# In-projection of a streaming-encoder layer: p1 and p2 of four pairs ahead of the other operands, and the 1/rms spread between products

## The chip, the core and the metric

The kernel runs on one core of a Trainium2 chip. The metric is device time in microseconds (us) of one execution. The engines of the core run side by side, each with its own queue in a fixed order: TensorE (PE, matmul), VectorE (DVE), ScalarE (ACT), GpSimd (POOL) and SyncE (SP, which here only issues DMA transfers).

## The reference

One layer on x of 1024 frames by 1024 channels, all float32. The part that the change touches is the first: RMSNorm and the combined input projection.

```python
h    = rms_norm(x, norm_mix_pre)          # x / sqrt(mean(x^2) + eps) * gain
proj = h @ w_in                           # 1024 x 1024 times 1024 x 4096
q, k, v, u, gates = split(proj, [512, 1024, 1536, 2048], axis=-1)
y_a  = chunk_band_attention(q, k, v, rel_bias) @ w_attn_out
y_b  = multiscale_pool(u, w_pool_group, pool_scale) @ w_pool_out
g_a, g_b = split(sigmoid(gates + b_gate), 2, axis=-1)
x = x + rms_norm((g_a * y_a + g_b * y_b) @ w_o, norm_mix_post)
x = x + rms_norm(conv_gated_ffn(rms_norm(x, norm_ffn_pre), ...), norm_ffn_post)
```

## The kernel before

The 4096 output channels of the in-projection are 32 blocks of 128 (0 to 3 q, 4 to 7 k, 8 to 11 v, 12 to 15 u, 16 to 31 gates), taken two at a time as 16 pairs (`IN_PAIRS`). A matmul multiplies 128x128 of weights with 512 frames. Each float32 factor is split into a high and a low part (`split`, L77): ScalarE casts the high part (L78), VectorE subtracts it from the source for the low part (L79); the product then takes three matmuls (high·high, high·low, low·high), and with four slices of the inner dimension one product is 12 matmuls (`mm3`, L81).

Pairs 0 and 1 are computed plainly, from x that only carries the gain (tiles XR, products named i); their outputs are scaled by 1/rms when they are evicted (`evict_first`). For that ScalarE sums the squares of the rows (`squares`), small steps make 1/rms, and `spread` lays it out along the frames: a broadcast copy bc, four TensorE transposes into a PSUM bank (rps), a copy to the tile R0 or R1 (one for each half of the frames). Then `normalise` scales the four quadrants of x (q, in the trace xq) in place, four VectorE steps for a quadrant.

From pair 2 on, a pair is a 2x2 block product by a scheme with seven products instead of eight (`Pair`). They need these operands, each split into a high and a low tile of 128 x 2048 (`operand`, two steps of 128x1024 on ScalarE and two on VectorE): B11 for p1, B21 for p2, T1 for p5, T2 for p6, B22 for p3, T3 for p7, T4 for p4. T1 to T4 are made by `sub` from the quadrants, in place, in two VectorE steps each. On the weights' side, p5, p6, p3 and p7 use sums s1, s2, s4 and s3 of the raw blocks (`first`, `sums`, 128x512, on GpSimd); the weights of a product are split as well (wh, wl). p1 goes to the PSUM bank X, p6, p7 and p4 are added onto it there, and after p1, p6 and p7 something is read from it (copies c1, u2; evictions), so that the next product waits for that reading. p5 goes to bank Y, p3 is added onto it; p2 goes to Z. There are two banks of each name, and two named m.

Queues: code order, then a scheduler that sets the order on each engine once, by priority and its own estimates; in the trace every engine follows its queue. Raw weights (win) are loaded by SP into six buffers; pair 4's load takes the place of quadrant xq00, so it can be issued only when the last `sub`, which reads that quadrant, is done. After the in-projection come the pooled path, attention and the feed-forward block, which the change doesn't touch.

The printed lines below are those that the rows of the profile name. In the trace the buffer numbers are left out: X_i is bank X of any pair, wl_i any low weight, s_i any weight sum, i the plain products.

Of the kernel before, what the change touches and what calls it, by code (L numbers as in the profile page):

```python
# [17 lines left out]
P = 128  # L18
# [19 lines left out]
IN_PAIRS = (  # L38
    [(16 + m, 24 + m) for m in range(4)]
    + [(8, 9), (10, 11)]  # L40
    + [(12, 13), (14, 15)]
    + [(16 + m, 24 + m) for m in range(4, 8)]
# [5 lines left out]
def trunk(ctx, tc, xn, xt, w_in, cols, bias, w_ao, w_pg, w_po, w_o, gains, w_up, w_dn, out):  # L48
# [113 lines left out]
    class Pair:  # L162
# [3 lines left out]

        def __init__(self, raw, T, psp, tmp, name, evict, np_=6):
            w = raw.rearrange("p (f q k c) -> p f q k c", f=2, q=2, k=4)
            self.w11, self.w12, self.w21, self.w22 = w[:, 0, 0], w[:, 0, 1], w[:, 1, 0], w[:, 1, 1]
            self.T, self.psp, self.tmp, self.name, self.evict, self.np_ = T, psp, tmp, name, evict, np_  # L170

# [15 lines left out]
        def first(self):  # L187
            self.s1 = self.st("s1")
            G.tensor_tensor(self.s1, self.w21, self.w22, ALU.add)  # L189

        def sums(self):
            self.s2, self.s4, self.s3 = self.st("s2"), self.st("s4"), self.st("s3")
            G.tensor_tensor(self.s2, self.s1, self.w11, ALU.subtract)  # L193
            G.tensor_tensor(self.s4, self.w12, self.s2, ALU.subtract)
            G.tensor_tensor(self.s3, self.w11, self.w21, ALU.subtract)  # L195
# [12 lines left out]

        def p2(self):
# [4 lines left out]
        def p6(self):  # L214
            self.u2 = self.pt("u2")
            self.prod(self.X, self.s2, "T2", False, "6")
            A.copy(self.u2, self.X)

# [11 lines left out]
        def p4(self, last):  # L230
            X, c = (self.bank("Z"), self.c7) if last else (self.X, None)
            self.prod(X, self.w22, "T4", last, "4")
            self.evict(1, 0, X, c)
# [59 lines left out]
    with ExitStack() as ph:  # L293
# [73 lines left out]

        def half_in(pi, t, i, tag):


            for f in range(2):
                if i == 0:
# [10 lines left out]
        def squares(j):  # L383
            for t in range(4 * j, 4 * j + 4):
                A.activation(sq, xts[t], AF.Square, accum_out=ssq[:, t:t + 1])

        def spread(j):

            s = slice(4 * j, 4 * j + 4)
            rstd_of(rst[:, s], ssq[:, s], tmp, 4)  # L390
# [124 lines left out]

        def pair_in(n):
            return Pair(raws[n], T, psp, tmp, f"i{n}", evict_in(IN_PAIRS[n]))

        vds, pd = {}, None
        for pi, fb in enumerate(IN_PAIRS):  # L520
# [7 lines left out]
            if pi == 0:  # L528
# [24 lines left out]
                for j in range(2):  # L553
                    for i in range(2):
                        normalise(i, j)
                evict_first(0, 1)
            elif pi == 1:
                pair, nxt = pair_in(2), pair_in(3)
                operand("B11", q[0, 0])
                pair.p1()  # L560
                operand("B21", q[1, 0])
                pair.p2()
                evict_first(1, 1)
                pair.first()
                sub(q[0, 0], q[0, 1], q[0, 0])
                operand("T1", q[0, 0])
                nxt.p1()
                nxt.p2()
                pair.sums()
                pair.p5()  # L570
                sub(q[0, 0], q[1, 1], q[0, 0])
                operand("T2", q[0, 0])
                operand("B22", q[1, 1])
                sub(q[0, 1], q[1, 1], q[0, 1])
                operand("T3", q[0, 1])
                sub(q[1, 0], q[1, 0], q[0, 0])
                operand("T4", q[1, 0])
            else:
                after = nxt if pi == 2 else pair_in(pi + 1) if pi + 1 < len(IN_PAIRS) else None
                run_pair(pair, after, (), pi < 4)  # L580
                pair = after
            if 5 <= pi < 7:
                for b in IN_PAIRS[pi - 1]:
# [658 lines left out]
```

## Time and profile before

| | us |
|---|---|
| median of 3 runs (lowest, highest) | 1282.94 (1281.66, 1283.02) |
| the profiled execution | 1282.71 |
| its span, first to last instruction | 1280.9 |
| TensorE busy | 1245.8 |
| VectorE busy | 900.7 |
| ScalarE busy | 672.2 |
| GpSimd busy | 326.7 |

A matmul of 512 columns starts 0.227 us after the one before it when nothing is in its way, though its own record lasts 0.39 us, since matmuls overlap. A stretch in which TensorE is slow is therefore seen best by the number of matmuls in it: 90 in 20 us is full. The mean granted clock over the span is 0.994.

### The profile page before, as it was taken

Reading aid. Unit: us, or ns where it says so; the run is one execution under the profiler, and the core shown is the slowest. Engines: PE = TensorE matmul, PEld = TensorE weight load, DVE = VectorE, ACT = ScalarE, POOL = GpSimd, SP = SyncE. Lnnn points to the kernel's source line nnn. Section 1 sums busy time; section 2 is a strip of 40 time slices with the busy share of each in tenths; the row PEclk is TensorE's granted clock in tenths of the full one; section 3 lists DMA queues with packets and bytes.
Section 4 is the critical chain, followed back from the end, with each engine's and each line's share of the span. In section 5 each row is a group of like instructions: output and inputs, shape, how many; then the busy total and the mean of one; then the engine's idle time right before and its main releaser. Section 6 shows DMA issues by size and latency. Waiting matters only on the chain.

```text
span 1280.9 us, 16339 instructions
## 1 busy us (share of the span) xinstructions
PE 1245.8 (97%) x5780; PEld 1030.3 (80%) x5780; DVE 900.7 (70%) x1439; ACT 672.2 (52%) x1171; POOL 326.7 (26%) x278
## 2 busy tenths in 40 slices
PE   7969999999999999999999999999999999999997
PEld 6748888887788888888887888888888887888786
DVE  5883354685477777854789766766666666899958
ACT  7743344655377775433556455455555454445553
POOL 0132312323155656100033342343343310000000
PEclk9989999999999999999999999999999999999999
DMA  9252142234788964622233212222221249302003
GB/s 365 82 207 105 44 179 82 112 115 169 235 255 244 274 218 160 247 94 83 83 124 139 99 66 83 99 70 79 99 74 66 99 158 369 122 17 100 33 1 132
DMA packets 55569, 172.35 MB, mean 135 GB/s; under 512 B 5440, under 2 KB 6080, under 8 KB 50496
## 3 DMA queue, kind: packets, MB, share of 16 engines
q1 hardware_dynamic: 49136, 156.63, 35.4%
q10 hardware_dynamic: 4608, 8.39, 1.7%
q0 software_dynamic: 1744, 6.29, 1.3%
q8 instruction: 45, 0.74, 0.3%
q14 instruction: 36, 0.29, 0.1%
HBM read 124.11 MB, written 47.19 MB: 134 GB/s over the span
## 4 chain that ended last, share of the span: by engine, by line
PE 87%; DVE 7%; issue 3%; ACT 1%; DMA 1%; POOL 0%; DVEq 0%; SPq 0%; ACTq 0%; POOLq 0%
PE X_u L85 16%; PE X_i L85 10%; PE X L85 9%; PE Y_u L85 8%; PE wops L928 7%; PE Y L85 6%; PE Y_i L85 5%; PE Z_u L85 4%; PE y L85 4%; PE ybp L85 3%; PE u L85 3%; PE i L85 3%; PE f L742 2%; PE Z_i L85 2%; PE tp L717 2%
## 5 line engine op out<-in xcount | busy, mean ns | idle before, releaser
L1004 DVE SCALAR_TENSOR_TENSOR hc<-hu,cv,hc 128x1022 f32<-128x1022 f32 (+1 forms) x88 | 115.9, 1321 | 35.3 <-ACT hc L999 35.3
L78 ACT CAST wh_u<-s_u 128x512 fp32r<-128x512 f32 x80 | 49.5, 618 | 78.3 <-PE Y_u L85 38.1
L79 DVE TENSOR_TENSOR wl_u<-s_u,wh_u 128x512 fp32r<-128x512 f32 x80 | 57.1, 714 | 40.1 <-ACT wh_u L78 40.0
L189 POOL TENSOR_TENSOR s_u<-wup 128x512 f32<-128x512 f32 x20 | 36.5, 1824 | 172.8 <-DMA wup<-in_w_up 127.0
L79 DVE TENSOR_TENSOR wl_i<-s_i,wh_i 128x512 fp32r<-128x512 f32 x56 | 40.7, 729 | 55.6 <-ACT wh_i L78 55.6
L78 ACT CAST wh_u<-wup 128x512 fp32r<-128x512 f32 x72 | 44.6, 622 | 61.5 <-PE Y_u L85 28.9
L78 ACT CAST wh_i<-s_i 128x512 fp32r<-128x512 f32 x56 | 34.8, 621 | 61.5 <-PE X_i L85 27.1
L193 POOL TENSOR_TENSOR s_u<-s_u,wup 128x512 f32<-128x512 f32 x20 | 28.1, 1405 | 137.5 <-DVE wl_u L79 137.5
L999 ACT ACTIVATE hc<-hu,cv 128x1024 f32<-128x1024 f32 x44 | 54.6, 1244 | 10.6 <-DVE hu L989 8.1
L78 ACT CAST wh_i<-win 128x512 fp32r<-128x512 f32 x46 | 28.2, 622 | 48.7 <-PE X_i L85 32.7
L79 DVE TENSOR_TENSOR wl_u<-wup,wh_u 128x512 fp32r<-128x512 f32 x72 | 50.3, 700 | 4.8 <-PE tp L285 2.0
L195 POOL TENSOR_TENSOR s_u<-wup 128x512 f32<-128x512 f32 x20 | 45.4, 2272 | 30.6 <-DVE wl_u L79 30.6
L79 DVE TENSOR_TENSOR ptl<-tp,pth 128x512 fp32r<-128x512 f32 (+3 forms) x80 | 43.7, 555 | 13.6 <-ACT pth L78 12.2
L696 POOL TENSOR_SCALAR pe<-pe,st 128x640 f32<-128x640 f32 (+2 forms) x64 | 43.1, 676 | 33.1 <-DVE st L695 28.4
L693 ACT ACTIVATE pe<-sm,st 128x640 f32<-128x640 f32 (+2 forms) x64 | 44.6, 697 | 6.4 <-DVE st L691 5.5
L189 POOL TENSOR_TENSOR s_i<-win 128x512 f32<-128x512 f32 x14 | 19.7, 1406 | 104.7 <-DMA win<-in_w_in 58.3
L1009 ACT ACTIVATE hc<-hc 128x1024 f32<-128x1024 f32 x22 | 23.4, 1064 | 40.9 <-DVE hc L1004 40.9
L79 DVE TENSOR_TENSOR wl_i<-win,wh_i 128x512 fp32r<-128x512 f32 x46 | 32.6, 713 | 16.4 <-ACT wh_i L78 16.4
L691 DVE CUSTOM_DVE_ANT_0 sm<-pst,bt 128x640 f32<-128x640 f32 (+2 forms) x64 | 40.7, 651 | 4.0 <-PE pst L675 1.6
L85 PE MATMUL ybp<-mx,wh_yb 128*128 128x512 f32 x128 | 43.3, 418 | 0.0
L78 ACT CAST pth<-tp 128x512 fp32r<-128x512 f32 (+3 forms) x80 | 37.1, 472 | 9.1 <-PE tp L717 6.8
L193 POOL TENSOR_TENSOR s_i<-s_i,win 128x512 f32<-128x512 f32 x14 | 20.7, 1478 | 80.8 <-DVE wl_i L79 80.7
(498 smaller groups left out, 4219.0 us busy)
## 6 DMA issues: line engine op xcount, KB each, us to landing
wup<-in_w_up SPq DMA_DIRECT2D x22, 1024.0 KB, 5.1
win<-in_w_in SPq DMA_DIRECT2D x14, 1024.0 KB, 5.5
g_d<-hc SPq DMA_DIRECT2D x20, 512.0 KB, 2.6
sig_d<-d ACTq DMA_DIRECT2D x32, 256.0 KB, 2.0
a<-g_d SPq DMA_DIRECT2D x8, 1024.0 KB, 6.2
b<-in_w_dn SPq DMA_DIRECT2D x8, 1024.0 KB, 8.7
x<-in_xn SPq DMA_DIRECT2D x8, 512.0 KB, 12.7
v_d<-vt SPq DMA_DIRECT2D x8, 512.0 KB, 3.2
```

The source lines that it names most:

```text
L78: A.copy(hi, src)
L79: (eng or V).tensor_tensor(lo, src, hi.bitcast(F32), ALU.subtract)
L85: nc.tensor.matmul(ps, a[i], b[i], start=start and i == 0 and p == 0, stop=stop and i == n - 1 and p == 2, skip_group_check=True,)
L189: G.tensor_tensor(self.s1, self.w21, self.w22, ALU.add)
L193: G.tensor_tensor(self.s2, self.s1, self.w11, ALU.subtract)
L195: G.tensor_tensor(self.s3, self.w11, self.w21, ALU.subtract)
L691: V.tensor_tensor_reduce(so, sv, bv, -1.0, 3e38, ALU.add, ALU.min, st[:, 0:1])
L693: A.activation(pe[:, :n], sm[:, :n], AF.Exp, scale=-1.0, bias=st[:, 0:1], accum_out=st[:, 1:2])
L696: G.tensor_scalar(pe[:, :n], pe[:, :n], st[:, 2:3], 1.0, ALU.mult, ALU.mult)
L928: nc.tensor.matmul(ps[:, 512 * c:512 * c + 512], a[k // 4][:, k % 4, sl], wo[k][b][:, 512 * c:512 * c + 512], start=k == 0 and x == 0, sto ...
L999: A.activation(c, hu, AF.Identity, scale=cv[:, C_CW + 88 + b:C_CW + 89 + b], bias=cv[:, C_CB + b:C_CB + b + 1])
L1004: V.scalar_tensor_tensor(c[:, n:], hu[:, :S - n], cv[:, w:w + 1], c[:, n:], ALU.mult, ALU.add)
```

## The change

`IN_PAIRS` takes the u blocks as pairs 4 and 5 and the v blocks as pairs 6 and 7; before it was the other way round. For pairs 4 and 5 the first half of their weights (128x1024, what p1 and p2 need) is loaded a second time into tiles of its own (w12), and p1 and p2 of both are computed (`p12`) behind those of pairs 2 and 3, before p5 of pair 2. p1's result is kept in c1, a tile in SBUF; p6 of these pairs starts a new X bank, and VectorE adds c1 when p5, p6 and p4 are read. The whole weights of these pairs are loaded as before, and their other products run in their old place. The operands T1 to T4 and B22 are made between products. The weight sums of pairs 2 and 3 are made by VectorE, not GpSimd. All squares are summed before the first spread; the copy R of each spread is made by VectorE, not ScalarE; each spread stands behind one or two half products of pairs 0 and 1, and the quadrants of the first half of the frames are normalised between the two spreads. The transposes of the values (v) move with their pairs, from behind pairs 5 and 6 to behind pairs 7 and 8.

```diff
 IN_PAIRS = (
     [(16 + m, 24 + m) for m in range(4)]
+    + [(12, 13), (14, 15)]
     + [(8, 9), (10, 11)]
-    + [(12, 13), (14, 15)]
...
+        def p12(self, w, c1):
+            self.early, self.c1 = True, c1
+            w = w.rearrange("p (q k c) -> p q k c", q=2, k=4)
+            Z = self.bank("m")
+            self.prod(Z, w[:, 0], "B11", True, "1")
+            A.copy(c1, Z)
+            Z = self.bank("m")
+            self.prod(Z, w[:, 1], "B21", True, "2")
+            self.evict(0, 0, Z, c1)
...
             self.prod(self.Y, self.s1, "T1", True, "5")
-            A.copy(self.c5, self.Y)
+            if self.early:
+                V.tensor_tensor(self.c5, self.Y, self.c1, ALU.add)
+            else:
+                A.copy(self.c5, self.Y)
...
-            A.copy(Rb[j], ps)
+            V.tensor_copy(Rb[j], ps)
...
-                squares(0)
+                with tc.high_priority():
+                    for j in range(2):
+                        squares(j)
+                        scales(j)
+                half_in(0, 1, 0, "Z", (0,))
                 spread(0)
-                squares(1)
-                half_in(0, 1, 0, "Z")
-                spread(1)
                 for n in range(2):
                     evict_first(n, 0)
-                half_in(0, 1, 1, "Z")
+                half_in(0, 1, 0, "Z", (1,))
+                half_in(0, 1, 1, "Z", (0,))
+                for i in range(2):
+                    normalise(i, 0)
+                spread(1)
+                half_in(0, 1, 1, "Z", (1,))
...
-                pair, nxt = pair_in(2), pair_in(3)
+                pair, nxt = pair_in(2, V), pair_in(3, V)
+                wh = []
+                for n in (4, 5):
+                    w = tmp.tile([P, 1024], F32, tag="o", bufs=4, name=f"w12_{n}")
+                    nc.sync.dma_start(w, w_in[n][:, :1024])
+                    c = out_tile(f"c1_{n}")
+                    wh.append((w, c))
                 operand("B11", q[0, 0])
                 pair.p1()
                 operand("B21", q[1, 0])
                 pair.p2()
+                nxt.p1()
                 evict_first(1, 1)
-                pair.first()
                 sub(q[0, 0], q[0, 1], q[0, 0])
+                nxt.p2()
                 operand("T1", q[0, 0])
-                nxt.p1()
-                nxt.p2()
+                early = []
+                for n in range(2):
+                    p = pair_in(4 + n, None)
+                    p.p12(*wh[n])
+                    early.append(p)
+                    if n == 0:
+                        pair.first()
+                        sub(q[0, 0], q[1, 1], q[0, 0])
+                        operand("T2", q[0, 0])
                 pair.sums()
                 pair.p5()
-                sub(q[0, 0], q[1, 1], q[0, 0])
-                operand("T2", q[0, 0])
                 operand("B22", q[1, 1])
                 sub(q[0, 1], q[1, 1], q[0, 1])
+            elif pi == 2:
+                nxt.first()
+                pair.p6()
                 operand("T3", q[0, 1])
+                pair.p3()
                 sub(q[1, 0], q[1, 0], q[0, 0])
+                nxt.sums()
+                pair.p7(False)
                 operand("T4", q[1, 0])
+                nxt.p5()
+                pair.p4(False)
+                pair = nxt
```

How it moves the queues, at three places. The numbers in the names tell tiles apart; i2 to i5 are pairs 2 to 5, a leading digit is the product (wl_6_i2 is the low weight of p6 of pair 2).

VectorE, from the sixth operand on, before: T2, B22, T3 and T4 with the steps that make them, and in between the first low weight of p6 of pair 2.

```order
L79 TENSOR_TENSOR T2l_623<-xq00_103,T2h_622 128x1024 x2
L79 TENSOR_TENSOR B22l_629<-xq11_106,B22h_628 128x1024 x2
L424 TENSOR_TENSOR xq01_105<-xq11_106,xq01_105 128x1024 x2
L424 TENSOR_TENSOR xq10_104<-xq10_104,xq00_103 128x1024
L79 TENSOR_TENSOR T3l_637<-xq01_105,T3h_636 128x1024 x2
L424 TENSOR_TENSOR xq10_104<-xq10_104,xq00_103 128x1024
L79 TENSOR_TENSOR T4l_645<-xq10_104,T4h_644 128x1024
L79 TENSOR_TENSOR wl_6_i2_656<-s2_i2_595,wh_6_i2_655 128x512
L79 TENSOR_TENSOR T4l_645<-xq10_104,T4h_644 128x1024
L79 TENSOR_TENSOR wl_3_i2_673<-s4_i2_596,wh_3_i2_672 128x512
```

The same stretch of VectorE's queue now, from T2 on.

```order
L79 TENSOR_TENSOR T2l_642<-xq00_103,T2h_641 128x1024 x2
L476 TENSOR_TENSOR d12_0_634<-m_i4_617,c1_4_487 128x512
L79 TENSOR_TENSOR wl_2_i5_667<-w12_5_488,wh_2_i5_666 128x512
L201 TENSOR_TENSOR s3_i2_687<-win2_279 128x512
L79 TENSOR_TENSOR wl_5_i2_694<-s1_i2_637,wh_5_i2_693 128x512
L79 TENSOR_TENSOR B22l_711<-xq11_106,B22h_710 128x1024 x2
L476 TENSOR_TENSOR d14_0_682<-m_i5_665,c1_5_490 128x512
L453 TENSOR_TENSOR xq01_105<-xq11_106,xq01_105 128x1024 x2
L195 TENSOR_TENSOR s1_i3_720<-win3_281 128x512
L79 TENSOR_TENSOR wl_6_i2_724<-s2_i2_685,wh_6_i2_723 128x512
L79 TENSOR_TENSOR T3l_741<-xq01_105,T3h_740 128x1024 x2
L79 TENSOR_TENSOR wl_3_i2_747<-s4_i2_686,wh_3_i2_746 128x512
```

The low weights of p5, p6 and p3 of pair 2 now stand one after each operand; between them lie evictions of pairs 4 and 5 and weight sums that were GpSimd's.

TensorE, at the end of p2 of pair 3 (the bank Z_i3), before and, in the second block, now; m_i4 are the banks of p1 and p2 of pair 4.

```order
L85 MATMUL Z_i3_574<-B21l_511,wh_2_i3_575 128x512
L85 MATMUL Z_i3_574<-B21h_510,wl_2_i3_576 128x512
L85 MATMUL Y_i2_601<-T1h_549,wl_5_i2_604 128x512
L85 MATMUL Y_i2_601<-T1h_549,wh_5_i2_603 128x512
L85 MATMUL Y_i2_601<-T1l_550,wh_5_i2_603 128x512
```

```order
L85 MATMUL Z_i3_572<-B21l_517,wh_2_i3_573 128x512
L85 MATMUL Z_i3_572<-B21h_516,wl_2_i3_574 128x512
L85 MATMUL m_i4_599<-B11h_491,wh_1_i4_600 128x512
L85 MATMUL m_i4_599<-B11l_492,wh_1_i4_600 128x512
L85 MATMUL m_i4_617<-B21h_516,wh_2_i4_618 128x512
L85 MATMUL m_i4_617<-B21l_517,wh_2_i4_618 128x512
L85 MATMUL m_i4_599<-B11h_491,wl_1_i4_601 128x512
```

Where p5 of pair 2 came, p1 and p2 of pair 4 come, and behind them those of pair 5; 48 matmuls now stand ahead of p5 of pair 2.

SP, behind the loads of pairs 2 and 3, now; before, pair 4's load stood there first.

```order
L597 DMA w12_4_485<-in_w_in 128x1024
L597 DMA w12_5_488<-in_w_in 128x1024
L488 DMA u_d_69<-d12_0_634 128x512
L488 DMA u_d_69<-d14_0_682 128x512
L328 DMA win4_718<-in_w_in 128x2048
L328 DMA win5_838<-in_w_in 128x2048
```

Two half loads and two stores of u stand ahead of the load of pair 4.

## Rows read from the trace of the kernel before

**Rows 1.** The page: busy us, share of the span and instructions of each engine.

```profile
PE 1245.8 (97%) x5780; PEld 1030.3 (80%) x5780; DVE 900.7 (70%) x1439; ACT 672.2 (52%) x1171; POOL 326.7 (26%) x278
```

**Rows 2.** Windows: length, busy us (count) of PE, PEld, DVE, ACT, POOL; clock; DMA share, GB/s.

```profile
40.00:60.00 20.00, 19.77 (x89) 15.91 (x88) 18.36 (x30) 14.40 (x20) 1.29 (x1) 1.00 0.18 67
60.00:80.00 20.00, 12.37 (x48) 8.33 (x46) 20.00 (x21) 12.86 (x17) 2.16 (x1) 0.94 0.19 62
80.00:100.00 20.00, 15.75 (x62) 12.86 (x63) 13.55 (x16) 7.30 (x12) 12.21 (x8) 0.80 0.75 279
100.00:120.00 20.00, 20.00 (x90) 16.57 (x89) 6.64 (x10) 7.85 (x13) 5.93 (x5) 1.00 0.29 106
```

**Rows 3.** TensorE's waits, 0 to 340 us: total us, times, longest.

```profile
PE X_i L85 <- DVE wl_i L79: 9.4, 2, 9.2
...
PE Z_i L85 <- DVE wl_i L79: 1.2, 1, 1.2
```

**Rows 4.** Windows of 5 us; the clock is the third column from the end.

```profile
75.00:80.00 5.00, 0.07 (x1) 0.00 (x0) 5.00 (x5) 3.00 (x3) 0.00 (x0) 0.77 0.22 39
80.00:85.00 5.00, 0.75 (x2) 0.65 (x3) 5.00 (x6) 1.18 (x2) 0.63 (x1) 0.50 0.95 347
85.00:90.00 5.00, 5.00 (x18) 3.93 (x17) 3.16 (x5) 1.11 (x2) 4.92 (x3) 0.70 0.96 364
```

**Rows 5.** The chain that ended last, 0 to 130 us: start, us, what.

```profile
53.21 2.27 DVE B11l L79 x2
...
67.14 3.37 DVE xq L424 x2
...
83.59 0.61 DVE wl_i L79
...
101.25 2.72 PE Y_i L85 x12
```

**Rows 6.** TensorE in order of time: start, us, instruction, idle before and releaser.

```profile
33.22 0.60 PE L395 MATMUL rps<-ident,bc 128*128 128x128 f32 x4
...
44.85 0.60 PE L395 MATMUL rps<-ident,bc 128*128 128x128 f32 x4
...
84.25 0.79 PE L85 MATMUL X_i<-T2h,wl_i 128*128 128x512 f32 x1 [9.18 <-DVE wl_i L79]
...
88.36 0.40 PE L85 MATMUL Y_i<-B22h,wl_i 128*128 128x512 f32 x1
...
101.09 0.39 PE L85 MATMUL Y_i<-B22h,wh_i 128*128 128x512 f32 x1
```

**Rows 7.** VectorE, ScalarE and GpSimd in order of time, columns as above.

```profile
33.85 0.59 ACT L397 COPY R<-rps 128x512 f32<-128x512 f32 x1 [2.78 <-PE rps L395]
34.47 2.48 DVE L408 TENSOR_TENSOR d<-i,R 128x512 f32<-128x512 f32 x4 [4.15 <-ACT R L397]
36.87 3.17 DVE L402 SCALAR_TENSOR_TENSOR xq<-xq,cv,R 128x512 f32<-128x512 f32 x3
...
44.14 0.43 DVE L392 COPY bc<-rst 128x512 f32<-128x512 f32 x1
...
49.28 2.73 DVE L402 SCALAR_TENSOR_TENSOR xq<-xq,cv,R 128x512 f32<-128x512 f32 x4
...
67.27 2.16 POOL L189 TENSOR_TENSOR s_i<-win 128x512 f32<-128x512 f32 x1 [20.45 <-ACT wh_i L78]
...
75.57 3.48 DVE L424 TENSOR_TENSOR xq<-xq,xq 128x1024 f32<-128x1024 f32 x3
```

**Rows 8.** Loads and stores (us to landing); GpSimd's second sum (ns, min/median/max).

```profile
win<-in_w_in SPq DMA_DIRECT2D x5, 1024.0 KB, 5.3
...
x<-in_xn SPq DMA_DIRECT2D x8, 512.0 KB, 12.7
...
DMA to landing us min/median/max: 2.6/3.2/4.5
...
L193 POOL TENSOR_TENSOR s_i<-s_i,win x3: 1291/1298/3907, 35.5 to 93.3; 128x512 f32<-128x512 f32 x3
```

More of the change, by code (lines that the diff above doesn't have):

```diff
@@ L162, in trunk, with __init__, weights @@
     class Pair:
-        def __init__(self, raw, T, psp, tmp, name, evict, np_=6):
+        def __init__(self, raw, T, psp, tmp, name, evict, np_=6, eng=G):
+            self.early, self.eng = False, eng
+            self.weights(raw)
+            self.T, self.psp, self.tmp, self.name, self.evict, self.np_ = T, psp, tmp, name, evict, np_
+        def weights(self, raw):
+            if raw is None:
+                return
             w = raw.rearrange("p (f q k c) -> p f q k c", f=2, q=2, k=4)
             self.w11, self.w12, self.w21, self.w22 = w[:, 0, 0], w[:, 0, 1], w[:, 1, 0], w[:, 1, 1]
-            self.T, self.psp, self.tmp, self.name, self.evict, self.np_ = T, psp, tmp, name, evict, np_
         def st(self, n):
@@ L215, in p6 @@
             self.u2 = self.pt("u2")
-            self.prod(self.X, self.s2, "T2", False, "6")
-            A.copy(self.u2, self.X)
+            if self.early:
+                self.X = self.bank("X")
+            self.prod(self.X, self.s2, "T2", self.early, "6")
+            if self.early:
+                V.tensor_tensor(self.u2, self.X, self.c1, ALU.add)
+            else:
+                A.copy(self.u2, self.X)
         def p3(self):
@@ L230, in p4 @@
         def p4(self, last):
-            X, c = (self.bank("Z"), self.c7) if last else (self.X, None)
+            X, c = (self.bank("Z"), self.c7) if last else (self.X, self.c1 if self.early else None)
             self.prod(X, self.w22, "T4", last, "4")
@@ L366, in split_in, with half_in @@
                 ws[pi, f, i] = split_w(w[:, f, i], f"i{pi}_{i}{f}", None, place)
-        def half_in(pi, t, i, tag):
-            for f in range(2):
+        def half_in(pi, t, i, tag, fs=range(2)):
+            for f in fs:
                 if i == 0:
@@ L542, in trunk @@
                     split_raw(i, 1)
-                squares(0)
+                with tc.high_priority():
[3 more added lines that the diff above has]
+                half_in(0, 1, 0, "Z", (0,))
                 spread(0)
-                squares(1)
-                half_in(0, 1, 0, "Z")
-                spread(1)
                 for n in range(2):
                     evict_first(n, 0)
-                half_in(0, 1, 1, "Z")
+                half_in(0, 1, 0, "Z", (1,))
[4 more added lines that the diff above has]
+                half_in(0, 1, 1, "Z", (1,))
                 half_in(1, 1, 0, "Y")
                 half_in(1, 1, 1, "Y")
-                for j in range(2):
-                    for i in range(2):
-                        normalise(i, j)
+                for i in range(2):
+                    normalise(i, 1)
                 evict_first(0, 1)
             elif pi == 1:
-                pair, nxt = pair_in(2), pair_in(3)
+                pair, nxt = pair_in(2, V), pair_in(3, V)
[5 more added lines that the diff above has]
+                    wh.append((w, c))
                 operand("B11", q[0, 0])
@@ L562, in trunk @@
                 pair.p2()
+                nxt.p1()
                 evict_first(1, 1)
-                pair.first()
                 sub(q[0, 0], q[0, 1], q[0, 0])
+                nxt.p2()
                 operand("T1", q[0, 0])
-                nxt.p1()
-                nxt.p2()
+                early = []
[7 more added lines that the diff above has]
+                        operand("T2", q[0, 0])
                 pair.sums()
                 pair.p5()
-                sub(q[0, 0], q[1, 1], q[0, 0])
-                operand("T2", q[0, 0])
                 operand("B22", q[1, 1])
                 sub(q[0, 1], q[1, 1], q[0, 1])
+            elif pi == 2:
+                nxt.first()
+                pair.p6()
                 operand("T3", q[0, 1])
+                pair.p3()
                 sub(q[1, 0], q[1, 0], q[0, 0])
+                nxt.sums()
+                pair.p7(False)
                 operand("T4", q[1, 0])
-            else:
-                after = nxt if pi == 2 else pair_in(pi + 1) if pi + 1 < len(IN_PAIRS) else None
-                run_pair(pair, after, (), pi < 4)
+                nxt.p5()
+                pair.p4(False)
+                pair = nxt
+            else:
+                after = early[pi - 3] if 3 <= pi < 5 else pair_in(pi + 1) if pi + 1 < len(IN_PAIRS) else None
+                if after is not None and after.early:
+                    after.weights(raws[pi + 1])
+                run_pair(pair, after, (), pi < 6)
                 pair = after
-            if 5 <= pi < 7:
+            if 7 <= pi < 9:
                 for b in IN_PAIRS[pi - 1]:
```

17 lines of the change are left out of this document (10 added, 7 removed).

## The prediction

> **What bounds the kernel now.** I read the page's first two blocks first: TensorE is busy 97% of the span, so time can only come from the few places where it isn't [rows 1]. The table by 20 us shows the largest that the change touches: a full window of 20 us holds 90 matmuls, those from 60 and from 80 us hold 48 and 62, the second at a granted clock of 0.80 [rows 2]. The list of waits names VectorE as the releaser, above all one wait of 9.2 us for a weight's low part (wl) [rows 3]. The windows of 5 us show what that wait does beside it: granted clock 0.77, 0.50, 0.70 and then full again [rows 4]. The chain of waits says why: from 53 to 84 us the end is set almost only by VectorE, which makes operand after operand, two steps of 128x1024 at a time, and TensorE enters it for a few matmuls only; from 84.25 us on the chain is TensorE alone, 2.72 us for a product of 12 matmuls [rows 5]. So this block is VectorE's, and everything behind it TensorE's: what the block saves arrives at the end, as long as nothing later waits.
>
> How much is lost: from 55.07 us (first matmul of p1 of pair 2) to 101.09 us (first of p3 of pair 3) TensorE does 11 products, 132 matmuls. At 2.72/12 = 0.227 us each that is 29.9 us; it takes 46.0. **16.1 us are lost**, about 14.3 of them waiting and 1.8 at the half clock: the ten matmuls behind the long wait take 4.1 us (84.25 to 88.36) instead of 2.3 [rows 6].
>
> **The change part by part.** The order of TensorE's queue shows that p1 and p2 of pairs 4 and 5 now stand ahead of p5 of pair 2. They need only B11 and B21, so the same 11 products become 15 in the block, and four fewer have to run behind it. No matmul is added or removed. The comparison is thus: before, the same work ends at 101.09 + 4 x 2.72 = 111.97 us. Where does it end after?
>
> *Before the block.* The first spread's transposes (rps0) now stand behind 12 instead of 5 matmuls of the first half product, 7 x 0.23 = 1.6 us later: 33.2 + 1.6 + 0.6 = 35.4 us instead of 33.8 [rows 6]. The copy to R0 goes from ScalarE (0.59 us there) to VectorE. No row shows this copy on VectorE; the nearest are a broadcast copy of the same size (0.43) and an eviction from PSUM (0.62), I take 0.6 as it also reads PSUM [rows 7]. The Trainium skill, "VectorE: DVE Perf Modes", section "Why PSUM operands drop a tier", lets fp32 from PSUM run at one element a cycle, an estimate of 512 / 0.96 GHz = 0.53 us; by it the sum would be 0.1 us shorter, and no row here shows it. Behind R0 VectorE does four evictions (2.4), eight normalise steps (0.68 each beside no GpSimd work, 5.4; before, three of them took 3.17 us while GpSimd made a weight sum, which now is on VectorE), and some 1.1 of small steps up to bc1: 36.0 + 8.9 = 45.0 us. TensorE reaches rps1, now three matmuls later than before, at 44.85 + 0.7 = 45.5: no wait, with 0.5 us to spare. While it transposes, VectorE makes s1 and s2 of pair 2 (1.2), then copies R1 (0.6), makes s4 (0.6), eight normalise steps (5.4) and two evictions (1.2): **B11l begins at 54.0 us, where it began at 53.1** [rows 5, 7].
>
> *The block on VectorE.* From B11l to the low weight of p5 of pair 3 (wl_5_i3) its queue now holds 22 steps of 128x1024 (1.135 each, 25.0 us), 13 low weights, 8 evictions and 5 weight sums of 128x512 (26 x 0.61 = 15.8 us): 40.8 us. The sums on VectorE have no row either; a low weight is the same shape and also reads SBUF twice, so 0.61. Bounds: 0.57, half of a 128x1024 step, and 0.85, half of the slowest such step in the trace; eight sums, -0.3 to +2.0 us. They replace GpSimd's, and one GpSimd sum beside two operand steps took 2.16 us and held those up from 2.27 to 3.37 [rows 5, 7]: with GpSimd out of the block that delay goes too. So wl_5_i3 is ready at 54.0 + 40.8 = 94.8 us, if VectorE never waits.
>
> *Does VectorE wait?* Its steps that need TensorE or ScalarE, walked in the order of its queue: d18_0 (p2 of pair 2 ends at 62.2, VectorE is there at 62.6), d19_0 (66.7 and 67.3), d12_0 (73.1 and 74.3), d14_0 (78.5 and 79.0), d18_1 (88.1 and 88.9), d26_1 (93.1 and 93.6). It is there last each time, by 0.4 to 1.2 us. ScalarE is not bound: it has 0.95 us per 128x1024 cast against VectorE's 1.135, and loses to VectorE everywhere but at p5's copy, where p3 of pair 2 waits some 0.6 us for it.
>
> *TensorE through the block.* It waits for the first wl (57.0 instead of 56.1: 1.2 us in all, B11l's half included), 1.0 before p1 of pair 4, 0.6 and 0.4 at p3 and p6 of pair 2, 0.3, then 1.3 + 0.5 at p6 of pair 3 and p7 of pair 2, 1.2 at p4 of pair 2 behind d26_1; about 6 us in total, the longest piece 1.3. From wl_5_i3 on three stretches of ten matmuls are left up to p3 of pair 3 (5 of pair 3, 4 of pair 2, 6 of pair 3): 94.9 + 3 x 2.27 = **101.7 us against 111.97: 10.3 us gained.** Behind it VectorE has one low weight (0.6) for each 2.72 us of TensorE, plus an eviction.
>
> *Costed at nothing, and by what cover.* (a) The two half loads for pairs 4 and 5 are issued on SP when TensorE is done with the old tiles, at about 35 and 38 us, with the queues quiet by then (DMA share 0.18 from 40 us on) [rows 2]; they are needed at 67 us. (b) SP now has the u stores of d12_0 and d14_0 ahead of pair 4's load. That load waits for the last operand's subtraction anyway: issued at 88.3 instead of 78.0 us. With 5.3 us to land (the median of these five; 12.7 was the median of the eight x loads at the start), 1.3 for GpSimd's sum (up to 3.9), 0.6 and 0.7 for the split it is done at 96.2, at worst 106; p5 of pair 4 wants it at 101.7 + 5.4 = 107.1 [rows 7, 8]. Without this cover each us would count. (c) The added evictions (p5, p6, p4 of pairs 4 and 5 now add c1 on VectorE, six of 0.6 us) lie where VectorE is busy 7 of 20 us [rows 2]. (d) The values of pairs 6 and 7 now fall together with the pooled path's start, in pair 9: four splits, one low weight, two pooled steps of 1.2, an eviction, the next low weight, 7.3 us of VectorE, against five products (13.6 us) before p5 of pair 10 wants it.
>
> The profiled execution took 1282.71 us, span 1280.9; the median of the runs is 1282.94. 1282.9 - 10.3 = **1272.6 us**.
>
> **The rivals.** *Clock.* The block now has many short idles where it had one long one. The rows speak against a fall: from 56 to 75 us TensorE had waits up to 1.24 us and stayed at 1.00, and the level fell only in the wait of 9.2 us [rows 3, 4, 6]. The Trainium skill, "TensorE: Matmul & The Clock Gate", section "A second HAM failure mode: psum-queue depth-cycling", says that short and frequent idles between groups of matmuls can swing the clock between its two levels; the trace does not show that here. Where it happens, one fall costs 4.1 - 2.3 = 1.8 us as in the ten slow matmuls; one to two falls give 1274.4 to 1276.3.
>
> *Given back later.* If the cover of (b) or (d) fails: a store of values takes 3.2 us to land and frees a tile that the pooled path writes; one such wait inside pair 9, or a load that lands like those at the start, costs 1 to 4 us [rows 8]: 1273.6 to 1276.6.
>
> *VectorE is not faster without GpSimd.* If what slowed the two operand steps to 3.37 us and the three normalise steps to 3.17 was not GpSimd but the traffic around them, it can meet more steps in the fuller queue. If all were hit: 11 pairs of 128x1024 by 1.1, 16 normalise steps by 0.37, 21 sums and low weights by 0.3: 24 us, 1297 us. From 10.3 / 24 = 43% of them on nothing is gained, from 54% on the kernel is slower; a quarter of the way past that is some 1288. Against it: in the same trace three subtractions from 75.57 us take 3.48 (1.14 each) with ScalarE and DMA at work and GpSimd still [rows 7].
>
> *It doesn't do what it says.* The order of the queues excludes most of that; what could remain is that VectorE, not the products, sets the block, which is already the forecast.
>
> **How the numbers follow.** Forecast 0.68; clock 0.10; given back 0.08; VectorE slowed so that about nothing is left 0.08 (1280.5 to 1285.5); slowed further 0.06. A measurement of this kernel can tell about 0.2%, 2.6 us. Faster 0.68 + 0.10 + 0.08 = 0.86, same 0.08, slower 0.06. The forecast's own bounds are -0.3 to +2.0 for the sums, 0.4 for the copies, and about 1.5 either way for a walk in which waits of 0.4 us decide: 1270 to 1275.5. With the clock and the given-back cases the range is 1269.8 to 1277.8.
>
> **What would show it.** Right: no wait of TensorE over 2 us between 55 and 105 us, granted clock 1.00 in all windows from 60 to 100, VectorE without a gap from 54 to 94, wl_5_i3 near 95 us, p3 of pair 3 at 101 to 103 us after four more products; GpSimd idle until about 95; from 110 us on 90 matmuls in each 20 us. Wrong: VectorE idle in the block (a dependency that I walked wrongly), a window below clock 0.9, or operand steps above 1.2 us with GpSimd idle; behind the block, a wait at p5 of pair 4 or in pair 9.

## The result, and the profile after

The changed kernel takes **1274.75 us** (median of 4 runs, 1273.87 to 1275.48) against 1282.92 in the 4 runs of the kernel before beside it: ratio 0.9938, 95% interval 0.9921 to 0.9955. Five more runs of it, beside nine of before, gave 1274.74 us and 0.9937 (0.9925 to 0.9950). It is 8.2 us faster; 10.3 were forecast.

The profiled execution took 1275.48 us, span 1273.7. It is the longest of its four; the first profiled execution of the later set (a2 below) took 1273.87. Both are used, to tell what belongs to the program from what belongs to one execution.

The table by 20 us, columns as in [rows 2]:

```profile
40.00:60.00 20.00, 19.36 (x87) 15.54 (x86) 19.90 (x33) 12.62 (x17) 0.00 (x0) 1.00 0.25 90
60.00:80.00 20.00, 19.34 (x85) 15.69 (x85) 20.00 (x25) 12.99 (x20) 0.00 (x0) 1.00 0.17 66
80.00:100.00 20.00, 17.75 (x72) 12.69 (x72) 18.71 (x23) 9.86 (x15) 4.51 (x3) 1.00 0.75 265
100.00:120.00 20.00, 20.00 (x90) 16.58 (x89) 9.05 (x14) 8.03 (x13) 9.81 (x7) 1.00 0.46 166
200.00:220.00 20.00, 19.13 (x90) 15.40 (x89) 13.30 (x22) 10.25 (x18) 3.44 (x3) 1.00 0.61 227
220.00:240.00 20.00, 19.63 (x86) 15.85 (x85) 15.68 (x21) 11.68 (x20) 6.55 (x5) 1.00 0.36 136
```

The two windows that held 48 and 62 matmuls [rows 2] hold 85 and 72, the granted clock stays at 1.00, GpSimd (fifth pair of columns) is still up to 80 us, and VectorE is busy for 58.6 of the 60 us from 40 to 100. The last two rows are a place where TensorE is now busy 19.13 and 19.63 us of 20 (the 90 of the first take in transposes, which are shorter than a matmul of 512 columns). Before, nothing was lost there:

```profile
200.00:220.00 20.00, 20.00 (x90) 16.57 (x89) 6.82 (x11) 9.40 (x16) 4.24 (x4) 1.00 0.18 68
220.00:240.00 20.00, 20.00 (x90) 16.49 (x89) 12.74 (x18) 10.06 (x17) 6.51 (x4) 1.00 0.41 145
```

TensorE's waits from 0 to 340 us (total us, times, longest). The one of 9.2 us [rows 3] is gone. Apart from the wait for the first weights at the start of the program (7.5 us, 7.1 before), none is over 1 us:

```profile
PE X_i L85 <- DVE d L476: 1.8, 2, 0.9
PE X_i L85 <- ACT u_i L243: 0.9, 2, 0.6
PE X_i L85 <- ACT wh_i L78: 0.8, 1, 0.8
PE m_i L85 <- DVE wl_i L79: 0.7, 1, 0.7
PE X_i L85 <- DVE wl_i L79: 0.6, 1, 0.6
```

The chain of waits, 30 to 110 us (start, us, what). It answers [rows 5]:

```profile
54.46 2.27 DVE B11l L79 x2
...
69.04 6.29 PE m_i L85 x27
...
86.44 2.27 DVE xq L453 x2
...
93.99 0.61 DVE d L476
...
102.35 2.72 PE Y_i L85 x12
```

Before, the chain from 53 to 84 us was VectorE almost alone. Now TensorE's early products (m_i) stand in it for 6.29 us: the two engines share the block.

**Where the time went.** I cut each profiled execution at four instants that its TensorE records show: the first matmul of p1 of pair 2 (A), the first of p3 of pair 3 (end of the block, B), the last matmul of the in-projection with T4l (C), and the first matmul of attention behind its wait (D). Four products are 4 x 2.72 = 10.88 us.

| kernel | median us | A | B - A | C - B | D - C | end - D |
|---|---|---|---|---|---|---|
| before | 1282.9 | 55.07 | 46.02 | 247.74 | 2.98 | 929.1 |
| changed | 1274.75 | 55.46 | 46.73 | 238.49 | 3.68 | 929.3 |
| changed, again (a2) | 1274.74 | 54.04 | 46.69 | 238.57 | 3.75 | 929.1 |
| value blocks first (e4) | 1271.86 | 54.33 | 46.71 | 236.42 | 2.98 | 929.1 |
| R on ScalarE (e5) | 1274.47 | 54.90 | 46.07 | 238.68 | 3.35 | 929.4 |
| both of these (e7) | 1271.36 | 54.50 | 46.28 | 236.43 | 3.16 | 928.9 |
| sums on GpSimd (e1) | 1275.23 | 54.92 | 47.24 | 238.71 | 3.08 | 929.5 |
| no early products (e2) | 1281.87 | 54.71 | 44.36 | 248.71 | 2.86 | 928.9 |
| spread of before (e3) | 1273.72 | 54.45 | 45.16 | 239.00 | 3.36 | 929.6 |
| early products alone (e6) | 1275.68 | 54.73 | 47.97 | 239.17 | 2.97 | 930.1 |
| e3 and e4 together (e8) | 1271.45 | 55.16 | 45.31 | 236.38 | 3.04 | 929.8 |
| values' low halves left out (e10) | 1273.58 | 55.44 | 46.78 | 237.15 | 3.23 | 929.2 |

The block takes 0.7 us longer than before and holds four products more: 10.2 us gained (10.88 - 0.71). The stretch behind it should have become 247.74 - 10.88 = 236.86 us and took 238.49: **1.6 us given back**, and 0.7 more at the start of attention (3.68 for 2.98). What comes after is the same in all kernels within 1.2 us.

### The profile page after: what moved, and what is told of

It is laid out like the page before. It is cut to its first block, busy times and chain, and to the rows that moved or that the text cites. A ratio compares the mean times of both kernels' runs of the same rounds, so it can differ in the third digit from the quotient of the medians.

```text
span 1273.7 us, 16331 instructions
## 1 busy us (share of the span) xinstructions
PE 1245.4 (98%) x5780; PEld 1030.3 (81%) x5780; DVE 907.6 (71%) x1455; ACT 667.3 (52%) x1163; POOL 313.9 (25%) x270
## 3 DMA queue, kind: packets, MB, share of 16 engines
q0 software_dynamic: 1744, 6.29, 1.3%
## 4 chain that ended last, share of the span: by engine, by line
PE 87%; DVE 6%; issue 3%; ACT 2%; DMA 1%; POOL 0%; DVEq 0%; ACTq 0%; SPq 0%; POOLq 0%
PE X_u L85 16%; PE X_i L85 9%; PE X L85 9%; PE Y_u L85 8%; PE wops L986 7%; PE Y L85 6%; PE Y_i L85 5%; PE Z_u L85 4%; PE y L85 4%; PE ybp L85 3%; PE i L85 3%; PE u L85 3%; PE f L800 2%; PE Z_i L85 2%; PE tp L775 2%
## 5 line engine op out<-in xcount | busy, mean ns | idle before, releaser
L1057 ACT ACTIVATE hc<-hu,cv 128x1024 f32<-128x1024 f32 x44 | 54.6, 1243 | 10.9 <-DVE hu L1047 8.5
L775 PE MATMUL tp<-ident,pe 128*128 128x128 f32 x240 | 37.2, 278 | 0.4
L800 PE MATMUL f<-ptl,vv 128*128 128x256 f32 x144 | 36.8, 287 | 0.0
```

Of the source, the lines that this page charges most:

```text
L775: nc.tensor.transpose(tp[:, c * P:(c + 1) * P], pe[:, b * P:(b + 1) * P], ident)
L800: nc.tensor.matmul(fo, vv[:, kb, e].rearrange("p a d -> p (a d)"), t[:, s], start=s == slots[0] and x == 0, stop=s == slots[-1] and x == 1)
L1057: A.activation(c, hu, AF.Identity, scale=cv[:, C_CW + 88 + b:C_CW + 89 + b], bias=cv[:, C_CB + b:C_CB + b + 1])
```

## The experiments

All are edits of the changed kernel. The first four ran side by side.

**a2: the changed kernel again.** 

> The changed kernel again, as the yardstick for the three runs beside it, whose expected differences are near one microsecond. Expected: 1274.7 us within 0.7, with the same two waits of TensorE behind the block (0.87 us at 218 us, 0.37 at 234) if they belong to the program; if they were an accident of one execution they are gone here.

Measured 1274.74 us (1273.87 to 1275.86). The two waits are there again, 0.52 us at 217 and 0.37 at 233, and C - B and D - C repeat within 0.1 us: the give-back belongs to the program. A came 1.4 us earlier; more on that at the end.

**e4: value blocks first.**

```diff
     [(16 + m, 24 + m) for m in range(4)]
-    + [(12, 13), (14, 15)]
     + [(8, 9), (10, 11)]
+    + [(12, 13), (14, 15)]
...
-            if 7 <= pi < 9:
+            if 5 <= pi < 7:
```

> The changed kernel with the four value blocks back in their old place (pairs 4 and 5) and the K blocks 12 to 15 in pairs 6 and 7, so that the values' splits come two pairs before the pooled path starts. Theory (values and pooled path falling together give back what the block gained): the two waits of TensorE in pairs 8 to 10 (0.87 and 0.37 us) are gone and 1.2 to 1.6 us come back: 1273.3 us. Rival (those waits come from how a load happened to land): they stay or move, and the time is that of the changed kernel within 0.5 us.

Measured **1271.86 us** (1271.22 to 1274.44), ratio to before 0.9918 (0.9904 to 0.9931): 2.9 us faster than a2, twice what I expected. (One of its four runs, 1274.44, lies in a2's range; e7 and e8, which hold the same edit, repeat the gain. The "K blocks 12 to 15" of the expectation are the u blocks.) C - B falls by 2.15 and D - C by 0.77. The cause stands in the changed kernel's order of time (start, us, instruction, idle before and releaser); SPq is SyncE issuing a transfer:

```profile
210.20 0.69 DVE L79 TENSOR_TENSOR wl_i<-s_i,wh_i 128x512 fp32r<-128x512 f32 x1
...
210.97 0.33 SPq L533 DMA_DIRECT2D wg<-in_w_pg  x1
211.88 0.32 SPq L509 DMA_DIRECT2D u<-u_d  x1
...
216.51 0.15 DVE L518 COPY pl<-u 128x1 f32<-128x1 f32 x1 [2.43 <-DMA u<-u_d]
216.59 1.22 DVE L519 TENSOR_TENSOR pl<-u 128x1023 f32<-128x1023 f32 x1
217.72 0.69 DVE L476 TENSOR_TENSOR d<-X_i,p_i 128x512 f32<-128x512 f32 x1
...
218.46 0.50 PE L85 MATMUL X_i<-T4h,wh_i 128*128 128x512 f32 x1 [0.87 <-DVE d L476]
```

VectorE stands still for 2.43 us, since the next step in its queue reads u1, the second input of the pooled path, whose load SyncE issued at 211.88 us. The eviction d that TensorE needs stands behind that step. What held the load back was the order of SyncE's queue. Ahead of it stands the load of wg, a small weight of the pooled path, into a buffer that the weight sums also use, and SyncE's own waits from 205 to 212 us (total us, times, longest) show that it stood there for a low weight of VectorE, the one at 210.20:

```profile
SPq L533 <- DVE wl_i L79: 4.1, 1, 4.1
```

u1's own tile comes from the same four buffers as those of the values, but the last store of the values had landed at 209.50 us. Without wg ahead of it the load could have gone out some 2.4 us earlier, about as much as VectorE waited; that is an estimate, no run swaps the two. In e4, as in the kernel before, the same load stands ahead of wg's; in e4 it is issued and used 35 us earlier, and the two windows are full:

```profile
177.12 0.32 SPq L509 DMA_DIRECT2D u<-u_d  x1
...
181.95 0.14 DVE L518 COPY pl<-u 128x1 f32<-128x1 f32 x1
```

```profile
200.00:220.00 20.00, 20.00 (x90) 16.54 (x89) 7.56 (x12) 9.73 (x18) 5.55 (x4) 1.00 0.34 109
220.00:240.00 20.00, 20.00 (x90) 16.32 (x89) 14.69 (x22) 11.44 (x20) 6.17 (x4) 1.00 0.36 136
```

Not all of the 2.15 us was a loss, though. In e4, e7 and e8 four of the values' 32 transposes run inside the block, ahead of B, where the changed kernel waits 0.36 us at p3 of pair 2; in the other kernels they come behind B, at 0.11 us each. In e4:

```profile
81.18 0.60 PE L501 MATMUL vps<-ident,vd 128*128 128x128 f32 x4
```

Those 0.44 us account for e4's C - B, 236.42, being below the 236.86 that nothing lost would give.

A wait costs more than the list of waits says. The list gives the gap to the end of the last record (0.87 us), but a record lasts 0.39 us where the next matmul would start after 0.23. The listed wait of 0.52 us in a2 is a step of 0.91 us from one start to the next, so 0.68 lost there, and the matmul behind it costs another 0.1.

**e10: the values' low halves left out.** GpSimd writes zeros in their place, so this kernel does not compute the low halves of v.

```diff
-                split(vt[:, :, :, 0, :], vt[:, :, :, 1, :], pv)
+                A.copy(vt[:, :, :, 0, :], pv)
+                G.memset(vt[:, :, :, 1, :].bitcast(F32), 0.0)
```

> The changed kernel with the low halves of the values not computed: GpSimd writes zeros in their place, so VectorE loses eight steps of 0.6 us in pairs 8 and 9, while the tiles, the stores and the order of the loads stay. It tells apart two causes of the waits in pairs 8 to 10. Theory (VectorE waits there for the load of the next pooled input, which SyncE can issue only behind the stores of the values and into a tile that they free): the load still goes out at about 210 us, VectorE still waits about 2 us for it, and the time stays within 0.7 us of the changed kernel's, 1274.0 to 1275.4 us. Rival (VectorE has too many steps there): the waits of TensorE at 211, 217 and 233 us go, 1272 to 1273 us.

Measured 1273.58 us (1272.65 to 1274.32), between the two. The load went out about where I expected it, but VectorE waited 0.29 us for it, not 2:

```profile
211.36 0.37 SPq L510 DMA_DIRECT2D u<-u_d  x1
...
215.03 0.15 DVE L519 COPY pl<-u 128x1 f32<-128x1 f32 x1 [0.29 <-DMA u<-u_d]
```

TensorE's waits in this place are gone, and C - B is 237.15: 1.4 of the 2.15 us that e4 regains. With the 0.44 us of the transposes, 0.3 are left open. Neither cause is the whole. This execution and the first one of the changed kernel began alike (A is 55.44 and 55.46 us), so their times compare directly. Here too SyncE stood at the load of wg until 210.9 us; u1's load was issued 0.5 us earlier and took 3.6 us to land instead of 4.5, and the step that reads u1 began 1.5 us earlier. How much the steps left out and the earlier landing are worth each by itself, and why the load landed sooner, stays open.

**e5: the copies R on ScalarE.**

```diff
-            V.tensor_copy(Rb[j], ps)
+            A.copy(Rb[j], ps)
```

> The changed kernel with the two copies of the spread 1/rms on ScalarE, as before the change. Theory (VectorE's queue sets the block from the normalise steps on): two steps of 0.6 us leave that queue ahead of B11l, which begins 1.0 to 1.2 us earlier, and all of it arrives at the end: 1273.6 us. Rival 1 (ScalarE is busy there and the copies come late, so that VectorE waits for them): no gain, 1274.7 us. Rival 2 (the block is TensorE's by now): B11l earlier, but TensorE waits no less: 1274.7 us.

Measured 1274.47 us (1274.18 to 1274.95): 0.3 us less than a2, not told apart from it. The block is 0.6 us shorter, but counted from the first spread's transposes B11l does not begin earlier (19.2 us behind their start, as in a2):

```profile
35.30 0.59 ACT L426 COPY R<-rps 128x512 f32<-128x512 f32 x1 [3.99 <-PE rps L424]
...
35.91 1.29 DVE L437 TENSOR_TENSOR d<-i,R 128x512 f32<-128x512 f32 x2 [6.54 <-ACT R L426]
...
53.85 2.35 DVE L79 TENSOR_TENSOR B11l<-xq,B11h 128x1024 fp32r<-128x1024 f32 x2
```

VectorE has nothing else to do before R0 (it idles 6.54 us), so that copy is in line with its work whichever engine makes it. Only the second copy leaves its queue, and the order fills that place with one more weight sum. My expectation counted both copies; one counted.

**e7: e4 and e5 together.** 

> Both edits together: value blocks in pairs 4 and 5, copies of 1/rms on ScalarE. If both theories hold the gains add, since they lie in different places: 1.2 to 1.6 and 0.6 to 1.2 us, 1272.3 us. If the block's gain is taken again by a wait behind it, as in the changed kernel, the time is that of the better one of the two alone.

Measured 1271.36 us (1270.99 to 1272.98), ratio 0.9914 (0.9901 to 0.9928): e4's gain, and 0.5 us more, within the spread.

**e1: the sums on GpSimd.**

```diff
-                pair, nxt = pair_in(2, V), pair_in(3, V)
+                pair, nxt = pair_in(2), pair_in(3)
```

> The changed kernel with the eight weight sums of pairs 2 and 3 on GpSimd again; all else as changed. Theory (a GpSimd sum beside a step that reads two SBUF operands holds VectorE's step up by about 1.1 us, as the one such place in the trace of before): VectorE's queue loses eight steps of 0.6 us, 4.8, and gets back up to 8 x 1.1 = 8.8; between 0.5 us faster and 4 us slower than the changed kernel, 1274.2 to 1278.7 us, and the trace shows operand steps and normalise steps far above 1.14 and 0.68 us beside each sum. Rival (the slow steps of before came from the traffic around them, GpSimd is free): up to 4.8 us off a queue that sets the block, 1270 to 1272 us.

Measured 1275.23 us (1274.60 to 1276.89): 0.5 us slower than a2, less than their spread; the block is 0.55 us longer. The theory's two terms are both there and nearly cancel. From its order of time:

```profile
83.42 1.77 DVE L79 TENSOR_TENSOR wl_i<-s_i,wh_i 128x512 fp32r<-128x512 f32 x1
...
86.25 3.45 DVE L453 TENSOR_TENSOR xq<-xq,xq 128x1024 f32<-128x1024 f32 x2
...
85.36 2.12 POOL L200 TENSOR_TENSOR s_i<-win,s_i 128x512 f32<-128x512 f32 x1 [0.72 <-DVE wl_i L79]
...
90.22 0.50 PE L85 MATMUL X_i<-T2h,wh_i 128*128 128x512 f32 x1 [1.72 <-ACT wh_i L78]
```

A low weight beside a sum takes 1.77 us instead of 0.68, two operand steps 3.45 instead of 2.36, and the sum 2.12 instead of 1.29: the rival, by which GpSimd was innocent, falls. The Trainium skill, "GPSIMD Engine Reference", section "1. Specifications", says that GpSimd's SBUF interfaces are shared with VectorE and that VectorE's instructions with two SBUF inputs contend for them; the trace agrees, since each of the steps slowed here reads two SBUF tiles.

**e2: no early products.** p1 and p2 of pairs 4 and 5 run in their own pairs; the order of the operands, sums and spread as changed. The lines not shown take out the two half loads and let pairs 4 and 5 begin with their own p1 and p2.

```diff
-                early = []
-                for n in range(2):
-                    p = pair_in(4 + n, None)
-                    p.p12(*wh[n])
...
-                after = early[pi - 3] if 3 <= pi < 5 else pair_in(pi + 1) if pi + 1 < len(IN_PAIRS) else None
+                after = pair_in(pi + 1) if pi + 1 < len(IN_PAIRS) else None
...
```

> The changed kernel without the early products: p1 and p2 of pairs 4 and 5 run in their own pairs again, so the block has 11 products as before the change, while the operands are still made between the products, the sums still lie on VectorE and 1/rms is still spread in mid-block. Theory (VectorE's queue sets the block, TensorE's products lie in its shadow): four products of 2.72 us, 10.9, go behind the block, and VectorE's queue gets shorter by four low weights and two evictions, 3.6 us: 7.3 us slower than the changed kernel, 1282.0 us, with one or more long waits of TensorE and the granted clock falling there. Rival (the other parts of the change hold the gain, the early products only fill time that would not be waited for): within 1.5 us of the changed kernel, 1273.5 to 1276.2 us.

Measured **1281.87 us** (1281.26 to 1283.38), ratio to before 0.9993 (0.9984 to 1.0002): as the theory had it, to 0.2 us. The block is only 2.3 us shorter for four products less. TensorE waits for the weights again, and its clock falls to the lower of its two levels:

```profile
71.14 0.79 PE L85 MATMUL Y_i<-T1h,wl_i 128*128 128x512 f32 x1 [3.99 <-DVE wl_i L79]
```

```profile
70.00:75.00 5.00, 3.86 (x9) 3.09 (x10) 5.00 (x6) 1.48 (x2) 0.00 (x0) 0.50 0.00 0
```

So the rest of the change without them is worth 1.2 us by the medians (1281.87 against 1283.08 beside it), not told apart from nothing: the interval takes in 1.

**e6: the early products alone.** The spread, the sums on GpSimd and the order of the operands are those of before.

```diff
-                pair, nxt = pair_in(2, V), pair_in(3, V)
+                pair, nxt = pair_in(2), pair_in(3)
...
-                    if n == 0:
-                        pair.first()
-                        sub(q[0, 0], q[1, 1], q[0, 0])
-                        operand("T2", q[0, 0])
                 pair.sums()
                 pair.p5()
+                sub(q[0, 0], q[1, 1], q[0, 0])
+                operand("T2", q[0, 0])
                 operand("B22", q[1, 1])
...
```

> The kernel before with the early products alone: p1 and p2 of pairs 4 and 5 in the block (and the changed order of the column blocks), but the spread of before, the sums on GpSimd and the operands made in the old order, all ahead of p6 of pair 2. Theory (VectorE's queue sets the block, so that products put into its shadow are free but for their own low weights and evictions): the long wait of 9.2 us at p6 of pair 2 shrinks by about the 10.9 us of products and grows by the 3.6 us of VectorE that they bring, the clock does not fall, and most of the gain is there: 1274.5 to 1277 us. Rival (without operands between the products TensorE waits as long as before, later): 1279 us or above, with a wait of more than 5 us.

Measured 1275.68 us (1275.01 to 1276.82), ratio 0.9943 (0.9929 to 0.9957): 7.4 us faster than before, within the theory's range. One clause of it was wrong: the wait at p6 of pair 2 is still 2.75 us and the clock does fall for a while.

```profile
85.98 0.50 PE L85 MATMUL X_i<-T2h,wl_i 128*128 128x512 f32 x1 [2.75 <-DVE wl_i L79]
```

```profile
85.00:90.00 5.00, 4.02 (x11) 3.19 (x12) 5.00 (x7) 1.68 (x3) 3.90 (x1) 0.68 1.03 433
```

**e3: spread and normalise order of before.**

```diff
-                with tc.high_priority():
-                    for j in range(2):
-                        squares(j)
-                        scales(j)
-                half_in(0, 1, 0, "Z", (0,))
+                squares(0)
                 spread(0)
+                squares(1)
+                half_in(0, 1, 0, "Z")
+                spread(1)
...
-            V.tensor_copy(Rb[j], ps)
+            A.copy(Rb[j], ps)
...
```

> The changed kernel with the spread of 1/rms and the order of normalising as before the change: the transposes behind few matmuls of the first half product, the copies on ScalarE, the scales of the second half in the second spread, both halves normalised at the end. Early products, operands between products and sums on VectorE stay. Theory (VectorE's queue sets the block, and before the change VectorE stood idle for 4.2 and 1.5 us ahead of the two spreads): three to four weight sums slip into that idle time and B11l begins 1 to 1.5 us earlier than in the changed kernel, 1272.7 to 1274 us: the new spread brings nothing by itself. Rival (the spread in mid-block is what lets VectorE begin the block in time): B11l later by 1 us or more, 1275.7 us or above.

Measured 1273.72 us (1273.38 to 1274.07), 1.0 us less than a2, as the theory had it.

```profile
33.86 2.48 DVE L438 TENSOR_TENSOR d<-i,R 128x512 f32<-128x512 f32 x4 [3.77 <-ACT R L427]
...
44.88 0.68 DVE L201 TENSOR_TENSOR s_i<-win 128x512 f32<-128x512 f32 x1
...
52.00 2.35 DVE L79 TENSOR_TENSOR B11l<-xq,B11h 128x1024 fp32r<-128x1024 f32 x2
```

All four sums of pair 2 begin before the second half is normalised, the last at 44.88 us, and B11l begins at 52.00 (52.95 in a2); the block is 1.5 us shorter. The later spread costs about a microsecond.

Beside e6 this run tells one thing more. Both have the old spread and the early products; e3 also has the sums on VectorE and the operands made between products. It is 2.0 us faster (the ranges lie apart) and its block 2.8 us shorter, so these two together are worth more here than the sums' 0.5 us in e1. The order of the operands was not run alone.

**e8: e3 and e4 together.** 

> The two edits that gained on the changed kernel together: value blocks in pairs 4 and 5, and the spread of 1/rms and the order of normalising as before the change; early products, operands between products and sums on VectorE stay. They lie in different places (ahead of the block, and in pairs 8 to 10), so that theory adds them: 1.0 and 2.9 us off 1274.7, 1270.8 us. Rival (what the block gains arrives as a wait behind it): that of the value blocks alone, 1271.9 us.

Measured 1271.45 us (1270.57 to 1271.78), ratio 0.9904 (0.9889 to 0.9919): 3.3 us faster than the changed kernel, where 3.9 was the sum. It and e7 beat both kernels and can't be told from each other.

## Why the prediction was right, and where it was 2 us off

The direction, the range and the mechanism held; the predicted 1272.6 us was 2.1 too low. Step by step:

- *VectorE sets the block, TensorE's products lie in its shadow.* Right, and shown from both sides: without the early products the gain is gone (e2), with them alone 7.4 of 8.3 us are there (e6).
- *B11l at 54.0 us, 40.8 us of VectorE to the last low weight, ready at 94.8.* 54.38 us, 40.7, 95.1 (rows below). VectorE had no gap.
- *TensorE waits about 6 us in the block, the longest 1.3.* 180 matmuls of 0.227 are 40.86 us; the block took 46.73: 5.9 lost where it was 16.1. The longest wait listed is 0.93 us.
- *p3 of pair 3 at 101.7 us, 10.3 gained.* 102.19 by the first record, against 111.97: 9.8 gained, 10.2 but for the 0.4 by which this execution reached A later.
- *R on VectorE 0.6, sums 0.61.* The record of each is 0.69 us; from start to start 0.73 for the first copy and 0.60 for the second.

```profile
35.85 0.69 DVE L426 COPY R<-rps 128x512 f32<-128x512 f32 x1 [5.90 <-PE rps L424]
36.58 1.89 DVE L437 TENSOR_TENSOR d<-i,R 128x512 f32<-128x512 f32 x3
...
46.68 0.69 DVE L426 COPY R<-rps 128x512 f32<-128x512 f32 x1
47.28 0.68 DVE L200 TENSOR_TENSOR s_i<-win,s_i 128x512 f32<-128x512 f32 x1
...
94.50 0.69 DVE L79 TENSOR_TENSOR wl_i<-s_i,wh_i 128x512 fp32r<-128x512 f32 x1
```

- The Trainium skill's "VectorE: DVE Perf Modes", section "Why PSUM operands drop a tier", from which I had estimated 0.53 us for that copy, came out low by 0.07 to 0.2 us: from start to start the copy takes what the other 128x512 steps around it take.
- *The spread in mid-block.* Costed at no wait, and there was none; but I gave it no price against the old order. e3 shows that it loses about 1.0 us: VectorE idles 5.90 us ahead of R0 in the changed kernel, and everything up to B11l stands behind that.
- *Cover (b), pair 4's load.* Held: its first sum begins at 95.33 us on GpSimd, p5 of pair 4 starts at 107.63 without a wait.
- ***Cover (d), pair 9: the step that failed.*** I set 7.3 us of VectorE's work against 13.6 us of TensorE's and saw room. The sum was of busy time only. Not in it was the order of SyncE's queue: u1's load stands behind wg's, which waits for a low weight of VectorE, so it goes out at 211.88 us only, and VectorE's queue stops at the step that reads it, with an eviction behind. It costs 1.6 us against before; against e4 the stretch is 2.15 us longer, 0.44 of them the transposes. The rival "given back later" had named this place and 1 to 4 us, at a chance of 0.08; the measured 1274.75 lies in its band, and still in the forecast's own, 1270 to 1275.5. The rival's cause, a store of the values that frees a tile late, is not what held the load: the last of them had landed 2.4 us before it went out.
- *Not in the sum at all: the start of attention.* TensorE's wait there grew by 0.8 us:

```profile
342.37 0.62 ACT L78 CAST hi<-d 128x512 fp32r<-128x512 f32 x1 [3.16 <-DMA q_d<-hi]
...
344.36 0.72 PE L742 MATMUL pst<-kh,qs 128*128 128x256 f32 x2 [3.07 <-DVE d L476]
```

  and before:

```profile
349.81 0.62 ACT L78 CAST hi<-d 128x512 fp32r<-128x512 f32 x1 [2.46 <-DMA q_d<-hi]
...
351.81 0.39 PE L684 MATMUL pst<-kh,qs 128*128 128x256 f32 x1 [2.25 <-DVE d L447]
```

  ScalarE waits for a store of q to land, 3.16 us against 2.46. In the other kernels D - C is anywhere from 2.86 to 3.36 us. The store isn't issued later: it goes out 7.4 us before C in every kernel. In the changed kernel it takes 9.0 us to land against 8.3 before, and the load of the values ahead of it in GpSimd's queue 9.2 against 8.6. Why these transfers take longer there is not settled.
- *The rivals.* Clock: the granted clock is 1.00 in every window of the block, through five listed idles of 0.36 to 0.93 us. The swings that the Trainium skill's "TensorE: Matmul & The Clock Gate", section "A second HAM failure mode: psum-queue depth-cycling", describes did not come, here or in e1. VectorE no faster without GpSimd: fell, two operand steps take 2.27 us of the chain, and e1 brings the slow ones back. Yet the net worth of moving the sums is only 0.5 us, since VectorE pays 0.6 for each.

## What to carry to other kernels

Where one engine sets a stretch, work of another that needs nothing new from it is nearly free there, and its price is what it puts into the setting engine's queue (here 3.6 us for 10.9). When work is moved away from one place, add up what it lands beside not only by busy time: look at what stands ahead of its loads in the issuing queue and what that waits for, and at what stands in the queue behind the step that will wait for the load. And of a bundle of edits, test each alone: here the early products made the gain, the sums on VectorE were worth half a microsecond, within the spread, the new spread cost about one and the new order of the column blocks gave back nearly three; the order of the operands, never run alone, is the part whose worth is still open.

## What the runs showed of the hardware

**TensorE's first matmuls run at half rate for a time that differs between executions, and the clock column doesn't show it.** The window from 10 to 15 us, in the changed kernel's first profiled execution and in a2:

```profile
10.00:15.00 5.00, 5.00 (x17) 3.92 (x16) 3.25 (x6) 2.92 (x6) 0.00 (x0) 1.00 1.04 416
```

```profile
10.00:15.00 5.00, 5.00 (x22) 3.99 (x22) 3.06 (x6) 3.32 (x6) 0.00 (x0) 1.00 1.02 405
```

The same program, 17 matmuls against 22, both under a clock of 1.00. In the order of time matmuls start 0.43 us apart up to 13.3 us in the one and up to 10.2 in the other, then 0.23. The trace's record of the clock begins only there, at 13.4 and 10.3 us, and the column counts the time before it as full. The 3.1 us more at 0.43 instead of 0.23 us a matmul make up the 1.4 us in A, and A most of the 1.6 us that separate these two executions; a difference of a microsecond between kernels is better read from the stages than from their ends.

**The clock and single waits.** It stayed at 1.00 behind e1's wait of 1.72 us, and fell to 0.68 in the window of e6's 2.75 us and to 0.50 behind e2's 3.99. In e2 it fell once more behind the next wait, 1.89 us at 79.15 us (0.66 in the window from 80 to 85).

**GpSimd and VectorE hold each other up, but not beside every step.** In e1 the sums beside steps of two SBUF inputs took up to 4.49 us; three that began from 34.39 to 37.12 us, while VectorE was idle or mostly evicted from PSUM, took 1.27 to 1.30. Which of the two pays differs: VectorE's two steps for B22l, beside the start of the sum of 4.49 us, took their usual 2.35 us, while beside the sum at 90.45 us, which took 1.30, two steps for T4l took 3.13.
